# Dividing the softmax exponentials by their sums on VectorE, in six of the eight heads of the first attention

## The chip, the cores and the metric

The kernel runs on one core of a Trainium2 chip. The metric is device time of one execution in microseconds (us); lower is better. The core has TensorE (PE; its weight loads are listed apart as PEld), VectorE (DVE), ScalarE (ACT), GpSimd (POOL) and SyncE (SP), which issues most of the DMAs here.

## The reference, cut to what matters

The program is a trunk of two layers over 512 frames of width 1024. Layer 0 is a multi-head latent attention (8 heads, block-causal in chunks of 64) and a SwiGLU FFN; layer 1 is a chunked attention (16 heads) and another FFN. Only the softmax of layer 0 and what follows from it matter here:

```python
s = (einsum('bqhd,bkhd->bhqk', qn, k_nope) + einsum('bqhr,bkr->bhqk', qr, k_rope)) * scale
s = where(mask, s, -inf)
p = softmax(s, axis=-1)
o = einsum('bhqk,bkhd->bqhd', p, v)
...
return o.reshape(B, S, MLA_HEADS * V_DIM) @ w_o
```

The softmax's division by the sum of a row may be done on `p` before the product with `v`, or on `o` after it.

## The kernel before, in words

All products run in fp32 as three matmuls (`mm3`, L355 to L358): each operand is kept as a high part and a low part, made by `split` (L143 to L145): ACT copies the source to the high part (L144), DVE subtracts it from the source for the low part (L145).

The first attention is written as 8 heads of 4 slots each (`attention`, L513). In the slot of head `h` and query tile `qt` (128 queries, `n` = 128, 256, 384 or 512 keys) `Head.scores` (L488) lets PE make the scores in a PSUM bank (tag `s`, 2 banks), DVE add the mask, scale and take the row's extreme (L494, `p` in SBUF), and ACT take the exponentials in place with their row sums (L496, the sum lands in one column of `sums`). Two slots later `Head.turn` (L500) transposes `p` on PE, 128x128 at a time, into a bank of tag `t` (2 banks, L508), and splits the result into `pth`, `ptl`. Two slots after a head's last scores `pv` in `start_a` (L1001) multiplies by the values: 12 matmuls into one bank `o` of tag `mm` (4 banks). The result has the head's features on the partitions and the queries in the columns, so the sums, which lie one to a partition, have to be turned before they can be multiplied in:

```python
V.reciprocal(sums, sums)                                      # L1009
of = U(name="of")
nc.scalar.copy(of, o)                                         # L1011
def rest():
    V.tensor_tensor(of, of, spread(sums), op=OP.mult)         # L1014
    oh, ol = U(F32R, "oh"), U(F32R, "ol")
    split(oh, ol, of)
    osp.append((oh, ol))
```

`spread` (L465) is four PE transposes of a broadcast column (L469) into a bank of tag `t`. `rest` is called one slot after `pv`.

Between the slots a filler (`fill_a`, L974) puts PE work that does not wait for the softmax: the values' second half, the projections of the next heads (`heads_a`), the second rotary part ahead of head 4's projections (`rotary(1)`, whose additions and products on DVE are L897 to L899), and after the last projection the first half of the output projection (`out_first`). Weights come by SP's DMA queue through `Feed` and are split like other operands (`whi`, `wlo`).

The order of instructions on each engine is not the order of the text. A planner of the framework sorts them by priority (their place in the text, moved up by `with first(n)`, L136) and by when it reckons them ready, once, when the program is built; on the chip each engine runs its list in order. SBUF tiles of 128x512 come from a pool of 39 (`U`).

Of the kernel before, what the change touches and what calls it, by code (L numbers as in the profile page):

```python
# [11 lines left out]
F32R = mybir.dt.float32r  # L12
I32 = mybir.dt.int32
AF = mybir.ActivationFunctionType
OP = mybir.AluOpType
# [3 lines left out]
D, S, P = 1024, 512, 128  # L19
# [49 lines left out]
def trunk(ctx: ExitStack, tc: tile.TileContext, a, out):  # L69
    nc = tc.nc  # L70
    V = nc.vector
# [10 lines left out]
    def name_(n):  # L82
        uid[0] += 1
        return f"{n}_{uid[0]}"

    def U(dt=F32, name="u"):
        return up.tile([P, S], dt, tag="u", name=name_(name), bufs=NU)
# [4 lines left out]
    def bank(tag="mm", name="b"):  # L92
        return ps.tile([P, S], F32, tag=tag, name=name_(name), bufs={"mm": 4, "s": 2, "t": 2}[tag])

    def small(name="sm"):
        return sp.tile([P, 4], F32, tag="small", name=name_(name))
# [38 lines left out]
    @contextmanager  # L135
    def first(n):  # L136

        tc.cur_priority -= n
        yield
        tc.cur_priority += n  # L140


    def split(dst_hi, dst_lo, src):  # L143
        return (nc.scalar.copy(dst_hi, src),  # L144
                V.tensor_tensor(dst_lo, src, dst_hi.bitcast(F32), op=OP.subtract))  # L145
# [5 lines left out]
    class Pair:  # L151
# [4 lines left out]
        def __init__(self, src):  # L156
            self.src, self.raw = src, {}
# [197 lines left out]
    def mm3(o, l, r, start, stop):  # L355
        nc.tensor.matmul(o, l[0], r[0], start=start, stop=False)  # L356
        nc.tensor.matmul(o, l[0], r[1], start=False, stop=False)  # L357
        nc.tensor.matmul(o, l[1], r[0], start=False, stop=stop)  # L358
# [106 lines left out]
    def spread(col, first=0):  # L465

        b = bank("t", "bc")
        for i in range(col.shape[1]):
            nc.tensor.transpose(b[:, (first + i) * P:(first + i + 1) * P],  # L469
                                col[:, i:i + 1].to_broadcast([P, P]), ident)  # L470
        return b
# [8 lines left out]
    class Head:  # L480

        def __init__(self, qk, bt, scale, pv, sums):
            self.qk, self.bt, self.scale, self.pv, self.sums = qk, bt, scale, pv, sums
            self.p, self.pt = {}, None

        def scores(self, qt):  # L488
            n = P * (qt + 1)
            sc = bank("s", "sc")  # L490
            self.qk(sc[:, :n], qt, n)
            p = U(name="p")
            mn = small("mn")
            V.tensor_tensor_reduce(p[:, :n], sc[:, :n], self.bt(n), scale=self.scale(qt), scalar=3e38,  # L494
                                   op0=OP.add, op1=OP.min, accum_out=mn[:, :1])
            nc.scalar.activation(p[:, :n], p[:, :n], AF.Exp, bias=mn[:, :1], scale=-1.0,  # L496
                                 accum_out=self.sums[:, qt:qt + 1])
            self.p[qt] = p

        def turn(self, qt):  # L500
# [273 lines left out]
    for k in range(KT):  # L774
        h, l = U(F32R, "xh"), U(F32R, "xl")
# [68 lines left out]
    for j in range(2):  # L844
        V.tensor_tensor(ckv[j], ckv[j], rkv, op=OP.mult)
        h, l = U(F32R, "ckh"), U(F32R, "ckl")
# [9 lines left out]
    for j in range(3):  # L856
        h, l = U(F32R, "cqh"), U(F32R, "cql")
        split_scaled(h, l, b2[j], g_q[:, j:j + 1])
        cqs.append((h, l))
    nsq = consts.tile([P, 4], F32, name="nsq")  # L860
# [10 lines left out]
    mask = pool[0].tile([P, S], F32, tag="mask", name="mask", bufs=1)  # L871
    nc.gpsimd.memset(mask, 0.0)
    nc.gpsimd.memset(mask[:64, S - 64:], -BIG)
    qr, qk_a, osp = {}, {}, []
# [113 lines left out]
    def start_a(h):  # L988
        fill.until(h)
        qh, ql, kh, kl = qk_a.pop(h)  # L990
        r = qr.pop(h)

        def qk(o, qt, n):
            q_ = slice(qt * P, (qt + 1) * P)
            nc.tensor.matmul(o, qh[:, q_], kh[:, :n], start=True, stop=False)
            nc.tensor.matmul(o, qh[:, q_], kl[:, :n], start=False, stop=False)
            nc.tensor.matmul(o, ql[:, q_], kh[:, :n], start=False, stop=False)
            nc.tensor.matmul(o, r[:, q_], kr1[:, :n], start=False, stop=False)
            nc.tensor.matmul(o, r[:, q_], kr2[:, :n], start=False, stop=True)

        def pv(pth, ptl):  # L1001
            fill.until("v")
            o = bank()
            v_ = slice(h * VD, (h + 1) * VD)
            for kt in range(NQT):
                q_ = slice(kt * P, S)
                mm3(o[:, q_], (va[kt][:, 0, v_], va[kt][:, 1, v_]), (pth[:, kt, q_], ptl[:, kt, q_]),
                    kt == 0, kt == NQT - 1)
            V.reciprocal(sums, sums)  # L1009
            of = U(name="of")  # L1010
            nc.scalar.copy(of, o)  # L1011
# [7 lines that stand above are left out]
            return rest  # L1019

        sums = small("sums")
        return Head(qk, lambda n: mask[:, S - n:], lambda qt: nsq[:, qt:qt + 1], pv, sums)

    firsts = []
    fill = Filler(fill_a())
    attention(H_A, start_a, fill, 13, 8 + 5 * 7 + 6 + 14, False)
    fill.drain()
    st.close()
# [474 lines left out]
    osp, qk_b, ofs, sums, biases = [], {}, {}, {}, {}  # L1503
# [196 lines left out]
```

## Time and profile before

| | |
|---|---|
| median of 3 runs | 1128.0 us |
| runs | 1127.02 to 1128.33 us |
| the profiled execution's own time | 1128.58 us |
| its span, first to last instruction | 1126.8 us |
| granted TensorE clock, mean | 0.998 of full speed |
| eight heads of the first attention, first to last L494 | 67.6 to 146.8 us of the span |

The span is the time between the first and the last instruction that the profile has; 1.78 us of the execution's own time lie around it. A matmul's duration in the list is its latency: the next one starts before it ends, so PE's rate is read from the distance between starts. Idle time of an engine that nobody waits for costs nothing.

### The profile page before, as it was taken

To read this page: it belongs to the slowest core of one execution; us is meant where nothing else is said; L and a number is where in the kernel's file an instruction comes from. 1 tells how busy PE (TensorE), PEld (TensorE's weight loads), DVE (VectorE), ACT (ScalarE), POOL (GpSimd) and SP (SyncE) were. 2 spreads that over 40 slices of the span, in tenths; PEclk is the share of its full clock that TensorE was granted. 3 is DMA by queue.
4 is the path that set the end of the run, shared out by engine and by line. 5 is a ranking of instruction groups with operands and counts; after the bars stand their busy time and mean duration, and the time that the engine had idled before them with its cause. 6 is when DMAs were issued, how large, how long until landed. Compare 5 with 4: busy or idle time off the path is not lost.

```text
span 1126.8 us, 18993 instructions
## 1 busy us (share of the span) xinstructions
PE 1109.3 (98%) x6973; PEld 984.4 (87%) x6973; DVE 932.5 (83%) x1671; ACT 685.3 (61%) x1339; POOL 69.6 (6%) x106
## 2 busy tenths in 40 slices
PE   9999999999999999999999999999999999999997
PEld 6788889999999998887888887779999999998885
DVE  7788737999899889978857977647999899889977
ACT  6476637755555566668536777546755555566675
POOL 2200000000000002400000000000000000002402
PEclk9999999999999999999999999999999999999999
DMA  7332125323332449861456656625323322459923
GB/s 235 110 110 81 70 76 205 132 89 99 105 103 95 140 150 256 138 205 41 165 150 172 154 153 159 170 86 184 134 92 95 113 94 95 141 168 286 171 58 76
DMA packets 62990, 150.85 MB, mean 134 GB/s; under 512 B 8432, under 2 KB 10224, under 8 KB 62896
## 3 DMA queue, kind: packets, MB, share of 16 engines
q1 hardware_dynamic: 55552, 136.61, 38.6%
q0 software_dynamic: 6912, 12.59, 6.8%
q8 instruction: 55, 0.90, 0.3%
q10 hardware_dynamic: 432, 0.44, 0.1%
q14 instruction: 39, 0.32, 0.1%
HBM read 119.52 MB, written 9.63 MB: 115 GB/s over the span
## 4 chain that ended last, share of the span: by engine, by line
PE 44%; DVE 5%; ACT 2%; issue 2%; DMA 1%; POOL 0%; POOLq 0%; DVEq 0%; ACTq 0%
PE al L1434 6%; PE b L356 6%; PE b L357 6%; PE b L358 6%; PE al L1185 4%; PE be L1434 4%; PE be L1185 3%; PE ga L1434 2%; PE pt L508 2%; PE de L1185 1%; PE ga L1185 1%; DVE wlo L145 1%; DVE raw L174 1%; DMA raw<-in_w_pair 1%; PE b L1558 1%
## 5 line engine op out<-in xcount | busy, mean ns | idle before, releaser
L144 ACT CAST whi<-raw 128x1024 fp32r<-128x1024 f32 (+3 forms) x224 | 225.5, 1008 | 227.3 <-PE al L1434 74.5
L145 DVE TENSOR_TENSOR wlo<-raw,whi 128x1024 fp32r<-128x1024 f32 (+3 forms) x224 | 260.7, 1165 | 63.0 <-ACT whi L144 61.2
L1434 PE MATMUL al<-th,whi 128*128 128x256 f32 x432 | 123.4, 286 | 0.2 <-DVE ut L1446 0.2
L1434 PE MATMUL al<-th,wlo 128*128 128x256 f32 x432 | 121.4, 281 | 0.0
L1434 PE MATMUL al<-tl,whi 128*128 128x256 f32 x432 | 121.1, 280 | 0.0
L356 PE MATMUL b<-xh,whi 128*128 128x512 f32 (+1 forms) x304 | 116.8, 384 | 0.2 <-ACT xh L148 0.2
L357 PE MATMUL b<-xl,whi 128*128 128x512 f32 (+1 forms) x304 | 113.3, 373 | 0.4 <-DVE xl L149 0.3
L358 PE MATMUL b<-xh,wlo 128*128 128x512 f32 (+1 forms) x304 | 112.8, 371 | 0.0
L174 DVE TENSOR_TENSOR raw<-raw,raw 128x1024 f32<-128x1024 f32 x72 | 86.5, 1218 | 1.3 <-DMA raw<-in_w_pair 1.1
L1434 PEld LDWEIGHTS al<-th,whi 128*128 128x128 f32 x432 | 81.4, 188 | 3.1 <-DVE ut L1446 1.2
L1434 PEld LDWEIGHTS al<-th,wlo 128*128 128x128 f32 x432 | 81.4, 188 | 0.3 <-DVE wlo L145 0.3
L1434 PEld LDWEIGHTS al<-tl,whi 128*128 128x128 f32 x432 | 81.4, 188 | 0.0
L496 ACT ACTIVATE p<-p,mn 128x128 f32<-128x128 f32 (+1 forms) x96 | 54.0, 562 | 31.8 <-DVE mn L494 31.6
L145 DVE TENSOR_TENSOR ptl<-pt,pth 128x128 fp32r<-128x128 f32 (+1 forms) x96 | 46.2, 485 | 28.8 <-ACT pth L144 23.2
L144 ACT CAST whi<-wd 128x512 fp32r<-128x512 f32 x86 | 49.9, 619 | 26.8 <-PE al L1185 11.9
L145 DVE TENSOR_TENSOR wlo<-wd,whi 128x512 fp32r<-128x512 f32 x86 | 56.3, 685 | 11.5 <-ACT whi L144 11.2
L358 PEld LDWEIGHTS b<-xh,wlo 128*128 128x128 f32 x304 | 57.4, 189 | 8.8
L357 PEld LDWEIGHTS b<-xl,whi 128*128 128x128 f32 x304 | 57.5, 189 | 8.5 <-DVE xl L149 1.9
L356 PEld LDWEIGHTS b<-xh,whi 128*128 128x128 f32 x304 | 57.6, 189 | 8.3 <-ACT xh L148 1.3
L144 ACT CAST pth<-pt 128x128 fp32r<-128x128 f32 (+1 forms) x96 | 40.3, 424 | 28.5 <-PE pt L508 27.8
L1185 PE MATMUL al<-whi,ph 128*128 128x512 f32 x132 | 51.9, 393 | 0.5 <-ACT y L1246 0.5
L1185 PE MATMUL al<-whi,pl 128*128 128x512 f32 x132 | 51.5, 390 | 0.0
(309 smaller groups left out, 3264.3 us busy)
## 6 DMA issues: line engine op xcount, KB each, us to landing
raw<-in_w_pair SPq DMA_DIRECT2D x72, 512.0 KB, 3.8
wd<-in_w_down SPq DMA_DIRECT2D x54, 256.0 KB, 5.8
raw<-in_w_o SPq DMA_DIRECT2D x16, 512.0 KB, 3.6
raw<-in_w_gu SPq DMA_DIRECT2D x16, 512.0 KB, 3.6
raw<-in_w_down SPq DMA_DIRECT2D x16, 512.0 KB, 4.3
raw<-in_w_qkb SPq DMA_DIRECT2D x16, 512.0 KB, 3.6
wd<-in_w_down POOLq DMA_DIRECT2D x22, 256.0 KB, 5.8
wd<-raw POOLq DMA_DIRECT2D x22, 256.0 KB, 4.3
```

The source lines that it names most:

```text
L144: return (nc.scalar.copy(dst_hi, src), V.tensor_tensor(dst_lo, src, dst_hi.bitcast(F32), op=OP.subtract))
L145: V.tensor_tensor(dst_lo, src, dst_hi.bitcast(F32), op=OP.subtract))
L174: V.tensor_tensor(t, x, y, op=OP.add)
L356: nc.tensor.matmul(o, l[0], r[0], start=start, stop=False)
L357: nc.tensor.matmul(o, l[0], r[1], start=False, stop=False)
L358: nc.tensor.matmul(o, l[1], r[0], start=False, stop=stop)
L496: nc.scalar.activation(p[:, :n], p[:, :n], AF.Exp, bias=mn[:, :1], scale=-1.0, accum_out=self.sums[:, qt:qt + 1])
L508: nc.tensor.transpose(t[:, kt * P:(kt + 1) * P], p[:, kt * P:(kt + 1) * P], ident)
L1185: nc.tensor.matmul(to[e], l[c], r[d], start=j < 4 and k == 0 and n == 0, stop=k == NF // 2 - 1 and n == 2, skip_group_check=True)
L1434: nc.tensor.matmul(o, l[c], r[d], start=first_ and n == 0, stop=k == K2 - 1 and n == 2, skip_group_check=True)
L1558: nc.tensor.matmul(o[:, q_], vv, pth[:, kt, q_], start=kt == 0, stop=False)
```

## The change

For the heads with `h >= 2`, each slot's exponentials are multiplied by the reciprocal of their sum on VectorE, in place, before they are transposed; the reciprocal is taken for one column at a time, and both instructions are moved up by 20 in priority. In `pv` these heads make no reciprocal of four columns, no copy of the bank, no `spread` and no product; `split` reads the bank itself, and is called in `pv` instead of in `rest`. Heads 0 and 1 stay as they are, and so does the second attention.

```diff
-        def __init__(self, qk, bt, scale, pv, sums):
-            self.qk, self.bt, self.scale, self.pv, self.sums = qk, bt, scale, pv, sums
+        def __init__(self, qk, bt, scale, pv, sums, whole=False):
+            self.qk, self.bt, self.scale, self.pv, self.sums, self.whole = qk, bt, scale, pv, sums, whole
...
             nc.scalar.activation(p[:, :n], p[:, :n], AF.Exp, bias=mn[:, :1], scale=-1.0,
                                  accum_out=self.sums[:, qt:qt + 1])
+            if self.whole:
+                r = self.sums[:, qt:qt + 1]
+                with first(20):
+                    V.reciprocal(r, r)
+                    V.tensor_scalar(p[:, :n], p[:, :n], r, None, op0=OP.mult)
             self.p[qt] = p
...
+            if whole:
+                oh, ol = U(F32R, "oh"), U(F32R, "ol")
+                split(oh, ol, o)
+                return lambda: osp.append((oh, ol))
             V.reciprocal(sums, sums)
             of = U(name="of")
             nc.scalar.copy(of, o)
...
-        return Head(qk, lambda n: mask[:, S - n:], lambda qt: nsq[:, qt:qt + 1], pv, sums)
+
+        whole = h >= 2
+        return Head(qk, lambda n: mask[:, S - n:], lambda qt: nsq[:, qt:qt + 1], pv, sums, whole)
```

## Rows read from the trace of the kernel before

**Rows 1.** The page: busy time by engine, and the chain that ended last.

```profile
PE 1109.3 (98%) x6973; PEld 984.4 (87%) x6973; DVE 932.5 (83%) x1671; ACT 685.3 (61%) x1339; POOL 69.6 (6%) x106
PE 44%; DVE 5%; ACT 2%; issue 2%; DMA 1%; POOL 0%; POOLq 0%; DVEq 0%; ACTq 0%
```

**Rows 2.** Busy time in stretches: from:to, us, then PE, PEld, DVE, ACT, POOL.

```profile
85.00:147.00 62.00, 61.43 (x358) 53.15 (x358) 45.28 (x109) 37.68 (x96) 0.00 (x0) 1.00 0.22 69
...
190.00:225.00 35.00, 35.00 (x258) 32.90 (x257) 34.81 (x87) 25.54 (x57) 2.16 (x2) 1.00 0.35 121
...
260.00:410.00 150.00, 150.00 (x1258) 148.82 (x1257) 138.12 (x191) 83.15 (x132) 0.00 (x0) 1.00 0.33 109
```

**Rows 3.** Timeline of PE in the first attention: start us, us, engine, line.

```profile
124.91 0.60 PE L469 MATMUL bc<-ident,sums 128*128 128x128 f32 x4
125.34 0.38 PE L508 MATMUL pt<-ident,p 128*128 128x128 f32 x2
...
148.71 0.60 PE L469 MATMUL bc<-ident,sums 128*128 128x128 f32 x4
149.14 0.38 PE L508 MATMUL pt<-ident,p 128*128 128x128 f32 x2
```

**Rows 4.** Groups between 60 and 170 us, and L1009: what `pv` and `rest` issue.

```profile
L1014 DVE TENSOR_TENSOR of<-of,bc 128x512 f32<-128x512 f32 x8 | 5.4, 681 | 3.0 <-ACT of L1011 2.6 <-PE bc L469 0.4
...
L1009 DVE RECIPROCAL sums<-sums x8: 171/177/179, 74.7 to 147.8; 128x4 f32<-128x4 f32 x8
...
L1011 ACT COPY of<-b 128x512 f32<-128x512 f32 x8 | 4.7, 584 | 5.8 <-PE b L358 5.8
...
L144 ACT CAST oh<-of 128x512 fp32r<-128x512 f32 x8 | 4.9, 616 | 0.7 <-DVE of L1014 0.7
...
L144 ACT CAST qh<-b 128x512 fp32r<-128x512 f32 x8 | 4.7, 581 | 1.0 <-PE b L358 1.0
...
L145 DVE TENSOR_TENSOR ol<-of,oh 128x512 fp32r<-128x512 f32 x8 | 5.5, 689 | 1.4 <-ACT oh L144 1.3
...
L145 DVE TENSOR_TENSOR ql<-b,qh 128x512 fp32r<-128x512 f32 x8 | 5.5, 690 | 2.3 <-ACT qh L144 2.2
```

**Rows 5.** Groups of DVE: products with a number, with a column, with a tile.

```profile
L806 DVE TENSOR_SCALAR rot<-rot 128x128 f32<-128x128 f32 x1 | 0.2, 226 | 0.0
...
L1356 DVE TENSOR_SCALAR g<-g 128x512 f32<-128x512 f32 x1 | 0.4, 420 | 0.0
...
L805 DVE TENSOR_SCALAR rot<-rot,inv 128x128 f32<-128x128 f32 x1 | 0.3, 286 | 0.0
...
L809 DVE TENSOR_TENSOR rot<-rot 128x128 f32<-128x128 f32 x1 | 0.3, 282 | 0.0
```

**Rows 6.** Busy time, heads 2 to 6, each from its first L494 to the next's.

```profile
85.17:94.84 9.67, 9.67 (x59) 8.57 (x58) 5.72 (x18) 5.15 (x15) 0.00 (x0) 1.00 0.16 55
94.84:111.88 17.04, 16.71 (x96) 14.00 (x94) 15.59 (x32) 11.19 (x25) 0.00 (x0) 1.00 0.36 84
111.88:118.03 6.15, 5.91 (x38) 5.04 (x38) 4.75 (x16) 3.98 (x12) 0.00 (x0) 1.00 0.50 197
118.03:128.00 9.97, 9.97 (x62) 8.81 (x61) 7.82 (x19) 6.79 (x17) 0.00 (x0) 1.00 0.15 54
128.00:138.10 10.10, 10.10 (x63) 9.00 (x62) 7.64 (x19) 6.95 (x17) 0.00 (x0) 1.00 0.15 52
```

**Rows 7.** Waits of PE's weight loads between 60 and 175 us: total, times, longest.

```profile
PEld b L356 <- DVE ra L897: 0.6, 1, 0.6
```

**Rows 8.** Timeline: head 5's last exponentials, their transposes, two reciprocals.

```profile
126.66 0.19 ACT L496 ACTIVATION_READ_ACCUMULATOR p<-p,mn 128x1 f32 x1
...
126.88 0.18 DVE L1009 RECIPROCAL sums<-sums 128x4 f32<-128x4 f32 x1
...
129.14 0.60 PE L508 MATMUL pt<-ident,p 128*128 128x128 f32 x4
...
147.80 0.18 DVE L1009 RECIPROCAL sums<-sums 128x4 f32<-128x4 f32 x1 [0.88 <-ACT p L496]
```

## The prediction, made before the changed kernel was run

> **What bounds the kernel now.** I read the page first: PE is busy for 98% of the span, and in the chain that ended last it has by far the largest share [rows 1]. A busy PE may still be one that waits inside, so I went on to the stretch that the change touches. From 85 to 147 us, where heads 2 to 7 run, PE is busy 61.43 of 62.00 us, while DVE has work for 45.28 and ACT for 37.68 [rows 2]. So in this stretch a cycle that PE needn't spend is a gain, and work given to DVE is free as long as DVE finds 16.7 us of idle time in the right places. What comes behind is no different: PE is busy 35.00 of 35.00 us from 190 on and 150.00 of 150.00 from 260 on [rows 2], so PE carries a head start on to the end. By head the room on DVE is very uneven: idle (length less DVE's busy time) are 3.95 us in head 2, 1.45 in head 3, whose stretch also holds the second rotary part, 1.40 in head 4, 2.15 in head 5 and 2.46 in head 6 [rows 6]. Heads 3 and 4 are also the only ones in which PE is not busy throughout (16.71 of 17.04, 5.91 of 6.15).
>
> **What goes.** Per changed head, four transposes of the sums leave PE. Their price is not the duration in the row (0.60 is the latency of the group), but the distance to the next start: 125.34 - 124.91 = 0.43 and 149.14 - 148.71 = 0.43 us [rows 3]; with the rounding of starts I take 0.44, 0.11 for each. Six heads give 6 x 0.44 = 2.64 us of PE. On DVE go the reciprocal of four columns, 0.18, and the product with the turned sums, 0.68, in all 0.86 us per head; on ACT the copy out of the bank, 0.58 [rows 4].
>
> **What changes its source.** The split now reads the bank in place of an SBUF tile. Rows of the same shapes price that: ACT's 0.616 from SBUF against 0.581 from a bank, DVE's 0.689 against 0.690 [rows 4]. That is nothing, on both engines. But the bank `o` is now held until DVE's subtraction is through, and no longer only until ACT's copy: one DVE instruction of 0.69 more, plus its queue. Behind it waits whoever wants the next `mm` bank, that is PE's filler. Nearest is the one wait of this kind in the stretch, 0.6 us, in which PE waited for DVE to be done with the rotary banks [rows 7]. The bounds are 0 (another of the four banks is free) and 0.6; I take 0, since in five of the six heads no row shows it.
>
> **What is added on DVE.** Per head there are four reciprocals of one column. The nearest row is the reciprocal of four columns, 0.177 [rows 4]; so short an instruction is nearly all fixed cost, so 4 x 0.177 = 0.71 us. Then four products of 128, 256, 384 and 512 columns with a column as the factor. The one row with such a factor is 0.286 at 128 columns; with a plain number 128 columns took 0.226 and 512 took 0.420, that is 0.065 for each 128 more; with a tile, 0.282 and 0.681 [rows 4, 5], 0.133 for each 128 more. If the column costs a fixed 0.06 and the slope is that of a plain number, the four take 0.286 + 0.351 + 0.415 + 0.480 = 1.53 us. If the column puts the instruction on the slope of a product of tiles, they take 0.286 + 0.419 + 0.552 + 0.685 = 1.94. At the prices of a plain number it would be 1.29. I take 1.53, as the operation is that of the plain-number rows and only the factor differs, and keep the ends. The net on DVE is 0.71 + 1.53 - 0.86 = 1.38 us per head (1.14 to 1.79), 8.3 us in all.
>
> Here a rule bears on the choice. The Trainium skill, in "VectorE: DVE Perf Modes", section "The perf-mode tier table", gives tensor_scalar two fp32 elements a cycle from SBUF and tensor_tensor one, and names both a constant and a per-partition column as its scalar. The row at 128 columns lies beside that of a product of tiles, so the trace does not yet bear the rule out for a column; by the rule the net is about 1.38 us per head, by the slope of tiles 1.79.
>
> **What hides it.** In heads 2, 5, 6 and 7 the idle time above covers 1.38 or 1.79 with room left (head 7 has what is left of the 45.28 us after 41.5 in heads 2 to 6, so 3.8 us of the last 8.9). In heads 3 and 4, 1.38 just fits 1.45 and 1.40; 1.79 would be over by 0.34 + 0.39 = 0.73 us, and PE would wait for that. Between 0 and 0.73 I take the middle, 0.35. The longer way from exponential to transpose (a reciprocal and a product, at most 0.18 + 0.69) lies within the two slots between them: in head 5 the last sum was there at 126.85, and the transposes that read it started at 129.14 [rows 8], 2.3 us later.
>
> **The added wait.** Each reciprocal waits on DVE for ACT's sum; behind it in DVE's list stand the next slot's L494 (which frees the score bank for PE), the low parts of the transposed exponentials and of the next head's queries and keys, and split weights. The planner, which places an instruction when it reckons its input ready, has put a reciprocal at 126.88, 0.03 us after the sum, and once left DVE waiting 0.88 us for it [rows 8]. The bounds are 0 and 0.88 for each; I take 0, because DVE has other work to put in between everywhere but at the very end, and the row of 0.88 is from that end.
>
> **Sum.** -2.64 + 0 + 0.35 + 0 = -2.29 us. From the profiled execution's own 1128.58 us (span 1126.8 and 1.78 around it) that is 1126.29. The median of the runs shown lies 0.58 below that execution, so against the median I predict 1128.0 - 2.3 = 1125.7 us. One bound for "no difference" is 0.2%, about what a measurement of this kernel can tell: 2.26 us, so 1125.74 to 1130.26. My forecast sits at its very edge.
>
> **Rivals.**
> - *DVE's idle time in heads 3 and 4 can't be used.* It consists of waits for ACT and PE, not of free slots; then all of the net there, 2 x 1.38 = 2.76, goes to PE: -2.64 + 2.76 = +0.1, 1128.1 us. For it: PE is short of full just there, and DVE is at 15.59 of 17.04 [rows 6]. Against it: a later DVE finds what it waited for already done.
> - *The reciprocals wait.* The mechanism is the added wait, in heads 3 to 6, with w us for each of four reciprocals: DVE is over by 4w + 1.38 less the idle time, summed over the four heads 16w - 1.95. From w = 0.29 on the gain is used up; slower by more than 2.26 from w = 0.43 on. With half the row's wait, 0.44, it is 5.1 - 2.64 = +2.5, 1130.5 us; with all of it, over 1138. Against it stands the planner; for it that ACT runs on the other side of every such wait and each slot now crosses between the two engines three times in place of two.
> - *The head start is lost behind.* From 190 to 225 us DVE is busy 34.81 of 35.00 [rows 2]. If it is DVE that paces there, PE only arrives earlier to wait: 1128.0. Against it: PE is full there too.
> - *More than the transposes.* ACT loses 0.6 us per head, and with a shorter way out of the heads the 0.57 us that PE is short of full in the stretch [rows 2] go as well: -2.64 - 0.57 = -3.2, 1124.8 us.
>
> **How the numbers follow.** The forecast gets 0.47, of which 0.39 lie beyond the 0.2% and 0.08 within; idle time that can't be used 0.17; the head start lost 0.08; the waiting reciprocals 0.20; more than the transposes 0.08. So faster 0.39 + 0.08 = 0.47, same 0.08 + 0.17 + 0.08 = 0.33, slower 0.20. The range reaches down to 1123.8, which is the last rival with a microsecond for what the order that the planner writes may do otherwise, and up to 1130.2, nearly to the waiting reciprocals at 0.44 us; the likeliest case by itself has 1124.8 to 1126.7.
>
> **What would show it.** Right: 8 instead of 32 transposes of sums; PE's stretch of the six heads shorter by about 2.6 us and still full; DVE's busy time there up by about 8 us; products of 512 columns near 0.48 us. Wrong: reciprocals with idle time ahead of them that ACT ended; matmuls of scores or of `pv` that wait for DVE in heads 3 and 4; a product of 512 columns near 0.68; or a difference that lies behind 170 us.

## The result, and the profile after

The changed kernel takes 1129.57 us (median of 20 runs, 1126.76 to 1131.75); the kernel before, in 20 runs beside it, 1127.49 (1126.06 to 1129.05). The ratio is 1.0016, 95% interval 1.001 to 1.0022, so about 1.8 us more where 2.3 less were forecast. The profiled execution took 1129.54 us of its own time, against 1128.58 before.

In the changed kernel the lines from L500 on lie 5 further on (L908, the rotary copies, is L913; L995 to L999, the scores, are L1000 to L1004); the new reciprocal is L501, the new product L502. First the page: busy time by engine, and the chain that ended last. Both answer to [rows 1].

```profile
PE 1107.1 (98%) x6949; PEld 983.1 (87%) x6949; DVE 938.7 (83%) x1707; ACT 682.6 (61%) x1333; POOL 70.1 (6%) x106
...
PE 49%; DVE 2%; ACT 1%; issue 1%; DMA 1%; POOL 0%; POOLq 0%; DVEq 0%; ACTq 0%
```

PE has 24 instructions fewer, as meant, and still the span is 1.0 us longer. The parts of the change are as costed. These are the groups of the changed kernel's VectorE between 60 and 175 us, then the transposes of sums that are left; they answer to [rows 4, 5]:

```profile
L145 DVE TENSOR_TENSOR ol<-b,oh 128x512 fp32r<-128x512 f32 x6 | 4.1, 688 | 3.4 <-ACT oh L144 3.4
...
L501 DVE RECIPROCAL sums<-sums 128x1 f32<-128x1 f32 x24 | 3.9, 161 | 4.9 <-ACT p L496 4.7
...
L502 DVE TENSOR_SCALAR p<-p,sums 128x512 f32<-128x512 f32 x6 | 2.9, 486 | 0.2
...
L502 DVE TENSOR_SCALAR p<-p,sums 128x384 f32<-128x384 f32 x6 | 2.5, 417 | 0.1
...
L502 DVE TENSOR_SCALAR p<-p,sums 128x256 f32<-128x256 f32 x6 | 2.1, 353 | 0.1
...
L502 DVE TENSOR_SCALAR p<-p,sums 128x128 f32<-128x128 f32 x6 | 1.7, 285 | 0.1
```

```profile
L469 PE MATMUL bc<-ident,sums x8: 272/272/273, 81.7 to 92.1; 128*128 128x128 f32 x8
```

Eight transposes instead of 32, and four products of 1.54 us together, where 1.53 was reckoned. So the loss is not in the price of the parts. Where it is, the windows say. The first of these of the changed kernel answers to [rows 2] (PE, PEld, DVE, ACT and POOL busy, PE's granted clock as a share, DMA share, GB/s):

```profile
85.00:147.00 62.00, 59.52 (x335) 51.41 (x334) 51.19 (x144) 36.02 (x91) 0.00 (x0) 0.97 0.23 69
...
107.00:110.00 3.00, 1.71 (x11) 0.97 (x9) 2.29 (x5) 2.83 (x7) 0.00 (x0) 1.00 0.41 96
110.00:111.60 1.60, 0.51 (x3) 0.31 (x3) 1.60 (x4) 1.55 (x4) 0.00 (x0) 1.00 0.50 117
111.60:113.00 1.40, 1.40 (x7) 1.26 (x8) 1.40 (x3) 0.00 (x0) 0.00 (x0) 0.82 0.83 253
113.00:114.50 1.50, 1.50 (x8) 1.50 (x8) 0.90 (x4) 0.49 (x2) 0.00 (x0) 0.50 1.01 399
114.50:116.00 1.50, 1.50 (x7) 1.50 (x6) 0.59 (x4) 0.60 (x2) 0.00 (x0) 0.53 0.17 66
```

PE is idle for 62.00 - 59.52 = 2.48 us of the stretch, against 0.57 before, and nearly all of that (1.29 + 1.09) lies between 107 and 111.6 us, ahead of head 4. Behind it the granted clock is at half, the lower of its two levels (1.2 GHz in place of 2.4), for 0.18 x 1.4 / 0.5 + 1.5 + 0.47 x 1.5 / 0.5 = 3.4 us. Three waits of the changed kernel between 60 and 175 us (engine, line and what it waited for: us in total, times, longest) name what PE waited for:

```profile
PE sc L1000 <- ACT kh L144: 1.7, 1, 1.7
...
PE b L356 <- DVE ql L145: 0.5, 1, 0.5
PE pt L513 <- DVE p L502: 0.3, 1, 0.3
```

The new products hold PE up for 0.3 us in all. The 1.7 are head 4's first scores, which wait for their own keys: ACT's copy of the projected keys out of its bank. Head 4's queries and keys had long been projected (the last product for the keys starts at 102.27 us); their split came late. ACT's list shows why. Before, from 106.9 us on:

```profile
106.93 0.59 ACT L144 CAST qh<-b 128x512 fp32r<-128x512 f32 x1
107.89 0.59 ACT L144 CAST pth<-pt 128x512 fp32r<-128x512 f32 x1 [0.38 <-PE pt L508]
108.38 0.59 ACT L144 CAST kh<-b 128x512 fp32r<-128x512 f32 x1
109.06 1.05 ACT L144 CAST whi<-raw 128x1024 fp32r<-128x1024 f32 x1
```

After:

```profile
108.02 1.05 ACT L144 CAST whi<-raw 128x1024 fp32r<-128x1024 f32 x1
109.01 0.59 ACT L144 CAST pth<-pt 128x512 fp32r<-128x512 f32 x1
109.49 0.59 ACT L144 CAST qh<-b 128x512 fp32r<-128x512 f32 x1
109.97 0.60 ACT L144 CAST kh<-b 128x512 fp32r<-128x512 f32 x1
```

The order is another. Before, the queries of head 4 (`qh`) stand ahead of head 3's last transposed exponentials (`pth`), and the keys (`kh`) right behind those. After, `qh` too stands behind `pth`, and the split of an output weight (`whi`), which is needed only later, ahead of all three. `kh` comes 1.59 us later: 1.12 because `pth` starts later, the rest because `qh` is between them. On PE this reads (changed kernel, timeline: start, us, engine, line; in brackets the idle time before):

```profile
108.34 0.63 PE L513 MATMUL pt<-ident,p 128*128 128x128 f32 x4 [0.26 <-DVE p L502]
110.62 0.50 PE L1000 MATMUL sc<-kh,qh 128*128 128x128 f32 x2 [1.65 <-ACT kh L144]
111.59 0.51 PE L356 MATMUL b<-pth,va 128*128 128x512 f32 x1 [0.47 <-DVE ql L145]
...
114.63 0.52 PE L1001 MATMUL sc<-kl,qh 128*128 128x384 f32 x1
114.95 0.52 PE L1002 MATMUL sc<-kh,ql 128*128 128x384 f32 x1
```

The first line is head 3's last transposes, which end at 108.97. ACT's `pth` waits for them, so it can't start before 109.0, and the weight's split only fills the time until then. PE's list has turned over, too. Before, the transposes start at 107.26, and between them and head 4's scores stand six products for head 5's keys (107.61 to 109.09 us) and one with head 3's values. After, the products for the keys stand ahead of the transposes, and nothing is left behind them. So PE runs dry for the 1.65 us that ACT needs after the transposes for `pth`, `qh` and `kh`, one behind the other. The next two lines are the waits; the values' product waits as well, for the low part of the queries, since the filler's banks are full of projections that nobody has split. The last two start 0.32 us apart; at the full clock scores of 384 columns start 0.17 apart.

Ahead of that turn of order something changes on DVE and SP. The second rotary part ends in 16 small copies on SP's queue that put the query tiles `qr` together. Its first and last copies and what follows, before:

```profile
98.13 0.51 SPq L908 DMA_DIRECT2D qr<-rh  x1
...
107.84 1.22 SPq L908 DMA_DIRECT2D qr<-rl  x2
```

After:

```profile
98.66 0.33 SPq L287 DMA_DIRECT2D raw<-in_w_o  x1
99.09 0.51 SPq L913 DMA_DIRECT2D qr<-rh  x1
...
109.37 1.22 SPq L913 DMA_DIRECT2D qr<-rl  x2
```

The last two are issued 1.53 us later. This goes back to DVE's work in head 3, into whose list ahead of the first `rl` a reciprocal, a product of 128 columns and a split (`ptl`) now fall: that `rl` starts at 99.10 instead of 98.14. (The second `rl` is no later, 102.39 against 102.45; but when it is ready the queue has 12 of the 16 copies left to issue, and before it had 9.) `qr`, and the queries and keys of head 4, are tiles of one ring of 15 (`A`, tag `a`), and head 4's stand behind the `qr` tiles in it. The theory: the later copies let the planner reckon head 4's tiles ready later, it puts the weight's split and head 3's `pth` first, and PE runs dry.

### The profile page after: what moved, and what is told of

It reads as the page before. It is cut to its first block, busy times and chain, and to the rows that moved or that the text cites. A ratio compares the mean times of both kernels' runs of the same rounds, so it can differ in the third digit from the quotient of the medians.

```text
span 1127.8 us, 18971 instructions
## 1 busy us (share of the span) xinstructions
PE 1107.1 (98%) x6949; PEld 983.1 (87%) x6949; DVE 938.7 (83%) x1707; ACT 682.6 (61%) x1333; POOL 70.1 (6%) x106
## 4 chain that ended last, share of the span: by engine, by line
PE 49%; DVE 2%; ACT 1%; issue 1%; DMA 1%; POOL 0%; POOLq 0%; DVEq 0%; ACTq 0%
PE al L1445 9%; PE b L356 6%; PE b L357 6%; PE b L358 6%; PE be L1445 5%; PE al L1196 4%; PE be L1196 3%; PE ga L1445 2%; PE pt L513 2%; PE de L1196 1%; PE ga L1196 1%; PE b L1569 1%; PE b L1570 1%; PE sc L1561 1%; PE sc L1562 1%
```

## The experiments

In each, the time is compared with runs of the kernel before on the same chip. Beside it stands a sum from the window 85 to 147 us of the trace, against [rows 2]: 0.11 us off for each transpose of sums left out, PE's idle time less the 0.57 of before, and half of the time at half clock. For the changed kernel it gives -2.64 + 1.91 + 1.70 = +0.97 us, and its profiled execution is 0.96 longer. So close a fit is luck: of the kernel with the first edit below, the profiled execution is 5.58 us shorter than that of the kernel before, and the sum is -3.1. The table at the end of this section has it for all runs.

**The `qr` tiles in a ring of their own**, in the changed kernel; the two rings together have as many tiles as the one had.

```diff
-        return pool[0].tile([P, S], F32R, tag="a", name=name_(name), bufs=15)
+        return pool[0].tile([P, S], F32R, tag="a", name=name_(name), bufs=10)
...
-            q = A("qr")
+            q = pool[0].tile([P, S], F32R, tag="r", name=name_("qr"), bufs=5)
```

> The changed kernel, but the rotated queries of heads 0 to 7 get a ring of their own (5 tiles) and the queries and keys of the heads keep a ring of 10, in place of one ring of 15 for both. Theory (the loss is where PE runs dry ahead of head 4, because ACT and DVE split a weight of the output projection ahead of head 4's queries and keys, which the planner holds back behind the 16 copies of the rotary part on SP): the queries and keys move up, no wait of PE over 0.5 us for L144's kh, no fall of the granted clock in the first attention, and the saving of the transposes stays whole: 1125.0 us, ratio to the kernel before 0.9975 to 0.9985. Rival 1 (the products on DVE as such cost PE 3.5 us in heads 3 and 4): no change against the changed kernel, ratio 1.001 to 1.002. Rival 2 (the loss lies in the clock alone and not in the order): PE still waits some 2 us, ratio about 1.000.

Measured: 1123.83 us, ratio 0.9976 (0.9967 to 0.9985). The window, and ACT's copies of head 4's queries and keys and the split of the next weight:

```profile
85.00:147.00 62.00, 61.87 (x349) 53.07 (x348) 51.87 (x145) 36.66 (x91) 0.00 (x0) 1.00 0.22 64
```

```profile
97.14 0.59 ACT L144 CAST qh<-b 128x512 fp32r<-128x512 f32 x1 [0.45 <-PE b L358]
...
101.56 0.58 ACT L144 CAST kh<-b 128x512 fp32r<-128x512 f32 x1
...
109.44 1.05 ACT L144 CAST whi<-raw 128x1024 fp32r<-128x1024 f32 x1 [0.16 <-PE b L357]
```

Keys are split 8 us earlier than in the changed kernel, PE is idle for 0.13 us of 62.00, the clock stays full, and the gain is there, with every added instruction on DVE still in place (51.87 us busy). Without the shared ring, what was added to DVE costs PE nothing in this stretch.

**The same ring in the kernel before.** This asks whether the ring alone is what gained.

```diff
-        return pool[0].tile([P, S], F32R, tag="a", name=name_(name), bufs=15)
+        return pool[0].tile([P, S], F32R, tag="a", name=name_(name), bufs=10)
...
-            q = A("qr")
+            q = pool[0].tile([P, S], F32R, tag="r", name=name_("qr"), bufs=5)
```

> The kernel before with the two rings, a control. Theory: it ran dry for some 0.4 us only ahead of head 4, so it gains at most that: ratio 0.9995 to 1.0005. If the rings alone are worth more (0.998 or less), what they give the changed kernel is not proof that the order there was the loss.

Measured: 1126.49 us, ratio 0.9998 (0.9989 to 1.0006). It isn't: PE was nearly full there already. So the ring gains only together with the change, which is then worth what the transposes are.

**The change from head 4 on only**, and from there a second time:

```diff
-        whole = h >= 2
+        whole = h >= 4
```

> The changed kernel with the new division from head 4 on (four heads in place of six). Theory: heads 2 and 3 have no more products on DVE around the second rotary part, the planner's list for ACT there is that of the kernel before, so no dry stretch, and four heads save 4 x 0.43 = 1.7 us: ratio 0.9980 to 0.9990. Rival 1 (products cost PE wherever DVE is near full, so head 4, too): ratio 0.9995 to 1.001. Rival 2 (the head start is lost behind): 1.000.

> The division from head 4 on once more, since its profile had PE ahead by 1.7 us behind the heads while its runs were hardly faster. Theory: 0.9980 to 0.9990, the first runs were at the slow end of a spread. Rival: 0.9995 again; then a part of the saving is lost in runs that the profile did not catch.

Measured: 1126.84 us, 0.9995 (0.9987 to 1.0004), and again 1126.98, 1.0001 (0.9992 to 1.001). Up to head 4's scores ACT's list is that of the kernel before, and in the heads PE gains as it should (idle 0.71 and 0.68 us of 62.00, so 16 x 0.11 less 0.1 = 1.6). But the gain isn't in the time, and both ratios lie above the range that was expected. Later, from 600 to 670 us, the scores of the second attention now wait for a copy of their keys; the waits of the two traces there, of which the kernel before has none:

```profile
PE sc L1561 <- DMA k<-f: 0.8, 1, 0.8
```

```profile
PE sc L1561 <- DMA k<-f: 1.0, 1, 1.0
```

That this wait is what takes the gain is likely and not shown: the first of the two traces, with its 0.8 us, is of an execution of 1125.61 us, 1.2 below the median of its own runs.

**In head 3 alone:**

```diff
-        whole = h >= 2
+        whole = h == 3
```

> The changed kernel with the new division in head 3 alone. Theory: its products are enough to turn the list over (weight ahead of head 4's queries), so nearly the whole loss of 3.5 us is there against a saving of 0.43: ratio 1.002 to 1.003, PE waits over 1 us for kh and the granted clock falls to half for some us. Rival (the loss grows with the number of products): about a sixth of it, ratio 0.9998 to 1.0005.

Measured: 1130.9 us, 1.0039 (1.0025 to 1.0052). One head of the six ends up slower than all six together, and slower than expected. The windows of this kernel:

```profile
85.00:147.00 62.00, 59.63 (x329) 51.51 (x328) 44.54 (x111) 35.69 (x90) 0.00 (x0) 0.94 0.23 68
...
110.00:113.00 3.00, 1.76 (x5) 1.48 (x6) 3.00 (x6) 2.16 (x5) 0.00 (x0) 0.70 0.62 139
113.00:116.00 3.00, 3.00 (x14) 2.90 (x13) 1.42 (x5) 0.74 (x3) 0.00 (x0) 0.50 0.68 255
116.00:119.00 3.00, 3.00 (x15) 2.93 (x14) 0.62 (x2) 1.39 (x5) 0.00 (x0) 0.66 0.00 0
```

The weight's split and `pth` stand ahead of head 4's queries here too, and PE waits the same 1.7 us for `kh`. Here ACT stands idle between the two, so the weight delays nothing:

```profile
109.62 0.58 ACT L144 CAST pth<-pt 128x512 fp32r<-128x512 f32 x1 [0.30 <-PE pt L513]
```

The clock is at half for 0.30 x 3 / 0.5 + 3 + 0.34 x 3 / 0.5 = 6.8 us, twice as long. That may not be the usual case: this trace is of the slowest of six executions, 1134.25 us. The added DVE work of one head is enough for the whole wait; DVE's busy time over the stretch, 44.54 us against 45.28, is no sign of it.

**Products and reciprocals left out.** Heads 2 to 7 keep the changed way out of the bank, and their outputs aren't divided.

```diff
             if self.whole:
-                r = self.sums[:, qt:qt + 1]
-                with first(20):
-                    V.reciprocal(r, r)
-                    V.tensor_scalar(p[:, :n], p[:, :n], r, None, op0=OP.mult)
+                pass
```

> The changed kernel without its reciprocals and products: heads 2 to 7 are not divided by their sums at all (this part of the computation is left out). What stays is the saving: 24 transposes, the copy and the product less. Theory: PE saves 6 x 0.43 = 2.6 us, the list of ACT puts the first of head 4's two operands ahead of the weight, the second behind it, so at most about 1 us is lost there and no long fall of the clock: ratio 0.9975 to 0.9988. Rival (the list turns over because the transposes went, not because of the products): PE waits over 1 us for kh, ratio 1.000 to 1.002.

Measured: 1125.8 us, 0.9984 (0.9975 to 0.9992). ACT's list has `qh` of head 4 ahead of the weight and `kh` behind it; PE's longest wait there is for the low part of the queries:

```profile
PE b L356 <- DVE ql L145: 0.6, 1, 0.6
```

So the order turns by half even here, where only work was taken away; but PE is idle for 1.13 us and no more, and the clock stays full.

**Products and reciprocals alone**, in the kernel before, with the reciprocal written to a tile that nobody reads and a product with a column of ones:

```diff
+            if self.whole:
+                with first(20):
+                    V.reciprocal(small("rx")[:, :1], self.sums[:, qt:qt + 1])
+                    V.tensor_scalar(p[:, :n], p[:, :n], ones, None, op0=OP.mult)
             self.p[qt] = p
```

> The kernel before with the added DVE work alone: for heads 2 to 7 a reciprocal of each column of sums into a scratch column, and a product of the exponentials with a column of ones in place; the way out of the heads stays that of before. Theory: the products turn the list over (weight ahead of head 4's queries) and nothing is saved: a dry stretch of about 2 us and a fall of the clock of 3 to 7 us at half, ratio 1.003 to 1.0045; DVE busy about 12 us more in the heads. Rival (products cost nothing as such, only together with the new way out): ratio 0.9995 to 1.0005.

Measured: 1131.59 us, 1.0037 (1.0025 to 1.0049). Window and waits:

```profile
85.00:147.00 62.00, 59.51 (x337) 50.95 (x336) 51.36 (x149) 36.82 (x92) 0.00 (x0) 0.97 0.23 69
```

```profile
PE sc L999 <- ACT kh L144: 1.7, 1, 1.7
```

The same wait, 1.65 us behind head 3's last transposes as in the change and in head 3 alone, and again 3.4 us at half clock. The whole loss of the change is that of its added DVE work, 4.2 us here; what it takes from PE gives back some 2.4 of them (from 1.0037 to 1.0016).

**All eight heads, with the ring of their own:**

```diff
-        whole = h >= 2
+        whole = True
```

> The two rings and the new division in all eight heads. Theory: two more heads save 2 x 0.43 us of PE, and heads 0 and 1 lie in a stretch where DVE is busier (9.9 of 10 us from 60 to 70), so up to 0.8 us may be lost there: ratio 0.9968 to 0.9980. Rival (DVE is the bound there): 0.998 to 1.000, with waits of PE for DVE ahead of 85 us.

Measured: 1123.13 us, 0.9971 (0.9959 to 0.9983), the fastest kernel here; the six heads with that ring lie within its interval. Some of what heads 0 and 1 give is lost again: from 147 to 190 us PE waits once for DVE's sum of squares, where before it doesn't, and with six heads 0.6 us:

```profile
PE tot L435 <- DVE acc L426: 1.6, 1, 1.6
```

**PE kept busy ahead of head 4.** Eight matmuls of 512 columns into a bank that nobody reads, behind head 3's last transposes, to part the wait from the fall of the clock:

```diff
+            if self.warm and qt == NQT - 1:
+                wb = bank("t", "wb")
+                for _ in range(8):
+                    nc.tensor.matmul(wb, cks[0][0][:, :P], cks[0][1], start=True, stop=True)
```

> The changed kernel with eight matmuls of 512 columns that nobody reads, into a bank of tag t, issued on PE right behind the last transposes of head 3, so that they lie where PE runs dry; every engine's list is otherwise that of the changed kernel there. It splits the loss in two: the wait for head 4's keys (kept) and the fall of the granted clock behind it (taken away, if it is PE's standing idle that brings it on). Theory: the granted clock stays at its upper level in the heads, PE's lag behind the kernel before at 114 us falls from 3.5 to about 1.8 us (1.7 us was 3.4 us at half clock), and behind the heads PE is level or ahead: ratio 0.9990 to 1.0002. Rival 1 (the fall has another cause): clock falls again, ratio 1.001 to 1.003. Rival 2 (the wait alone is the whole loss): the clock holds, ratio still 1.001 to 1.002.

Measured: 1128.93 us, 1.0007 (0.9999 to 1.0016), outside the ranges of the theory and of both rivals. As far as head 4's first scores the lists of ACT and DVE are those of the changed kernel. The matmuls fill the hole, and head 4's scores start behind them with no wait:

```profile
108.05 2.11 PE L520 MATMUL wb<-ckl,ckh 128*128 128x512 f32 x8
110.00 0.39 PE L1004 MATMUL sc<-kh,qh 128*128 128x128 f32 x2
```

The clock stays full from 110 to 119 us, so in the changed kernel it fell because PE was idle. In the heads the sum is better than the changed kernel's by 1.65 us. The time doesn't show it: in the trace, as in those of the kernel with the change from head 4 on, PE waits for a copy of keys in the second attention, 1.0 us at `sc` of L1567, and the interval overlaps the changed kernel's. How much of the loss in the time is the clock's stays open.

**Eight of the 16 copies on POOL's queue**, in the changed kernel:

```diff
-                    nc.sync.dma_start(q[d:d + 32].bitcast(F32),
+                    (nc.gpsimd if half and i else nc.sync).dma_start(q[d:d + 32].bitcast(F32),
```

> The changed kernel with half of the 16 copies of the second rotary part issued by POOL's queue in place of SP's; nothing else is edited, the ring of 15 stays. Theory (head 4's queries and keys stand behind these copies, one after the other on SP at some 0.6 us each): they move up, no wait of PE for kh over 0.5 us, no fall of the clock, ratio 0.9970 to 0.9988. Rival (the copies have nothing to do with it, it is DVE's load): as the changed kernel, 1.001 to 1.002. Slower copies on POOL's queue could make head 4's scores wait for their rotated queries: then PE waits for DMA at L1003.

Measured: 1126.03 us, 0.9986 (0.9977 to 0.9995). SP's last copy is issued at 103.34 us and POOL's last at 105.31, instead of 109.37, and ACT splits head 4's queries and keys well ahead of the weight:

```profile
103.61 0.57 ACT L144 CAST qh<-b 128x512 fp32r<-128x512 f32 x1
104.08 0.59 ACT L144 CAST kh<-b 128x512 fp32r<-128x512 f32 x1
...
107.86 1.06 ACT L144 CAST whi<-raw 128x1024 fp32r<-128x1024 f32 x1
```

PE is idle for 0.42 us. Rings and DVE's work are those of the changed kernel, so it is through these copies that the added work reached head 4: by way of the planned order, and not by a wait for them on the chip, since the changed kernel splits `qh` at 109.49 us, before the last two copies have been issued (109.37 to 110.59). The Trainium skill, "DMA: Bandwidth & Descriptors", section "Issuing engines are not separate DMA queues", says that starting transfers from several engines saves only the time to start them, which is usually small beside the transfer. Here it isn't small: a start takes some 0.6 us, against a median of 2.0 us from issue to landing, and 16 of them stand in a row for 11 us. With half of them on POOL's queue the row ends 4 us sooner, and the next head's casts come 6 us sooner.

**The changed kernel again,** with no edit, beside the last two:

> The changed kernel itself, on the chip and beside the runs of before of the two others. Theory: 1.001 to 1.0025, and the runs fall into two groups by their mean granted clock, those of 0.999 near or below the kernel before, those of 0.997 and less some 2 to 4 us above it.

Measured: 1128.89 us, 1.0009 (1.0 to 1.0017), a little below the range, with the same wait of 1.7 us and the same 3.4 us at half clock in the trace. The two takes lose 1.8 and 1.0 us, and the second's interval reaches down to nothing. The two groups by clock did not come out: in the first 20 runs the three with a mean clock of 0.999 are indeed the shortest (1126.76 to 1127.61 us), but here three with 0.999 took 1126.97, 1129.38 and 1129.87, and two with 0.997 took 1127.22 and 1127.34. So the clock alone does not explain the spread of the runs.

All runs; the sum as told above, the time as (ratio - 1) x the median of before:

| run | transposes less | PE idle, 85 to 147 us | us at half clock | sum, us | time, us (95%) |
|---|---|---|---|---|---|
| the change | 24 | 2.48 | 3.4 | +1.0 | +1.8 (1.1 to 2.5) |
| the change, again | 24 | 2.48 | 3.4 | +1.0 | +1.0 (0 to 1.9) |
| own ring | 24 | 0.13 | 0 | -3.1 | -2.7 (-3.7 to -1.7) |
| own ring, all heads | 32 | 0.17 | 0 | -3.9 | -3.3 (-4.6 to -1.9) |
| own ring, kernel before | 0 | 0.45 | 0 | -0.1 | -0.2 (-1.2 to 0.7) |
| from head 4 | 16 | 0.71 | 0 | -1.6 | -0.6 (-1.5 to 0.5) |
| from head 4, again | 16 | 0.68 | 0 | -1.6 | +0.1 (-0.9 to 1.1) |
| head 3 alone | 4 | 2.37 | 6.8 | +4.8 | +4.4 (2.8 to 5.9) |
| no products | 24 | 1.13 | 0 | -2.1 | -1.8 (-2.8 to -0.9) |
| products alone | 0 | 2.49 | 3.4 | +3.6 | +4.2 (2.8 to 5.5) |
| PE kept busy (8 x 0.21 us of matmuls added) | 24 | 0.82 | 0 | -0.7 | +0.8 (-0.1 to 1.8) |
| two queues | 24 | 0.42 | 0 | -2.8 | -1.6 (-2.6 to -0.6) |

In eight of the twelve, three terms from one window and the measured time lie within 0.9 us of each other. In three of the other four (from head 4, both takes, and PE kept busy; 1.0 to 1.7 us apart) PE waits for keys in the second attention, 0.8 to 1.0 us; what holds the two queues back, 1.2 us, no wait of PE shows. Head 3 alone waits for keys there too, 1.6 us, which its sum does not have. Each sum is from one execution, and some are far from the median of their kernel: head 3 alone was traced at 1134.25 us (median 1130.9), the two queues at 1124.53 (1126.03). So a part of the agreement, and of what is missing, is chance.

## Why the prediction was wrong

The measured time lies within the range, but on the other side of no change. By the prediction's own parts:

- **What goes: right.** 24 transposes left, and with PE full (own ring) the time is 2.7 us shorter, where 2.64 was reckoned.
- **What is added on DVE: right.** Products of 285, 353, 417 and 486 ns against 286, 351, 415 and 480; 128 more columns cost 67 ns, near the 65 of a plain number and far from the 133 of a product of tiles. The rule that the prediction weighed is in the Trainium skill, "VectorE: DVE Perf Modes": section "The perf-mode tier table" gives tensor_scalar in fp32 from SBUF twice the rate of tensor_tensor, and section "Scalar operands", not the table, says that the scalar may be a constant or one value per partition. The trace agrees for the column, 486 ns at 512 columns against 681 for a product of tiles. The reciprocals took 161 ns, not 177. Net per head 4 x 0.161 + 1.54 - 0.86 = 1.32 us, forecast 1.38.
- **What changes its source, and the bank held longer: right.** The split out of the bank took 688 ns on DVE, and no wait for a bank that the subtraction of `o` holds shows among PE's.
- **The added wait: right in its outcome.** Reciprocals wait for ACT in 10 of 24 cases, 4.7 us in all. The rival set one wait for every reciprocal of heads 3 to 6; there they wait 1.87 us in 6 of 16 cases, so its w is 0.12, far below the 0.29 from which on it had the gain used up. With the ring of its own reciprocals still wait 3.7 us, in 7 cases, and PE is idle for 0.13. So that the measured time, 1129.57, lies near that rival's 1130.5 is chance. (Its upper end mixes two starting points: from the 1128.0 that gave 1130.5, all of the row's wait gives 1137.5 and not over 1138.)
- **What hides it: the step that failed.** It put the cost of the added DVE work in heads 3 and 4 between 0 and 0.73 us, as a delay that PE would see, and took 0.35. Measured are 1.91 us more of PE idle in the stretch, nearly all of it ahead of head 4, and 1.70 from the half clock behind it, together 3.6. DVE's load is no measure of it: one head's added work, in head 3 alone, makes the same wait, and with the ring of its own all of the added work makes none. The step looked for a later end of the instructions that were there, in the order that stood in the trace. The added work turned the order over, in the lists that the planner writes, and the wait came out on another engine, at ACT's `kh`. What was late next was to be named, and wasn't: `ra` and `rl`, the 16 copies on SP behind them, and the `qr` tiles in one ring with head 4's queries and keys. The trace of before had the copies on SP's queue, from 98.1 to 109.1 us with nothing between them, and the prediction didn't read that queue. The same step took the way from exponential to transpose as covered, from a row of head 5 with 2.3 us in it. In head 3 the trace of before has only 0.59 us (sum there at 106.67, transposes at 107.26):

```profile
106.48 0.19 ACT L496 ACTIVATION_READ_ACCUMULATOR p<-p,mn 128x1 f32 x1
...
107.26 0.60 PE L508 MATMUL pt<-ident,p 128*128 128x128 f32 x4
```

With reciprocal and product it is 0.87 (107.47 to 108.34). PE pays 0.26 us of that directly; but ACT's `pth` waits for these transposes, and both of head 4's casts now stand behind `pth`.

- **The fall of the clock** was in no part. In the traces it is a second price on one wait, 1.70 us beside 1.91.
- **The rivals.** *DVE's idle time in heads 3 and 4 can't be used* falls with the ring of its own: there all the added work stands, and PE is full. *More than the transposes*, 1124.8 us with the 0.57 us of idle gone as well, is what the ring brings out (-3.1 by the sum). *The head start is lost behind* did not hold for the ring: of 3.1 us the time keeps 2.7, and PE is full from 190 to 225 us. It held for a small part ahead of that, the 0.6 us at L435, and perhaps for the change from head 4 on, at a place that the prediction didn't look at, behind 600 us, where PE waits for a transfer and not for DVE.

Shown by the runs: that the added DVE work makes the loss, that it comes by way of the copies and the shared ring, and that the clock falls because PE is idle. Argued only: that within the planner it is the reckoned time of the ring's tiles that puts head 4's casts last; its reckoning is not in a trace. Not tried on the chip: to change the order alone, with nothing else; nor the added instructions without their move up by 20 in priority, so that the move and the work are not told apart.

## What to carry to other kernels

Where a planner writes the order, an added instruction can cost more than its time: look up what the engine's next results feed (copies on a queue, tiles of a shared ring) and which of the next stage's tiles stand behind them. Compare the order of the lists before the durations: here a cast on ACT had moved behind another, and the products on PE that would have covered the wait had moved ahead of it. Ask of each entry that moved ahead whether its engine would have been idle there anyway, as ACT would in place of the weight's split. And an edit that lost as a whole can be a good one with a bad neighbour: with the `qr` tiles in a ring of their own the same change gives 0.24% (0.15 to 0.33).

## What the runs showed of the hardware

- 2.2 to 2.4 us of PE idle, spread over 4.6 us and with 1.65 as its longest piece, was followed by 3.4 us at half clock in three traces of two kernels (the change twice, products alone), and 2.1 us by 6.8 in the trace of a third (head 3 alone). With the hole filled by matmuls that nobody reads the clock stayed full.
- A product with a column costs some 0.06 us more than with a plain number, at 128 columns (285 against 226 ns) as at 512 (486 against 420), and no more for each column.
